# Output projection as seven block products, and the ends of the two down stages reordered, in a one-core decoder block

## The chip, the cores and the metric

The kernel runs on one core of a Trainium2 chip. The time is that of one execution on the device in microseconds (us); the profile is taken in one more execution by the hardware profiler. Lower is better. All arithmetic is float32 in value: each operand of a matrix product is split into a high part in the format fp32r and a low part, the rest, and a product is three matmuls (high by high, high by low, low by high).

## The reference

One decoder block over 512 tokens of 1024 features: a SwiGLU feed-forward, a token mixer, and a second SwiGLU feed-forward, each with an RMS norm before and after it and a residual. Cut to what matters:

```
f = swiglu(rms_norm(h, ffn1_pre_g), ffn1_w_gu, ffn1_w_down)        # d_ff 2816
h = h + 0.5 * rms_norm(f, ffn1_post_g)
u = rms_norm(h, mix_pre_g);  z = u @ w_in
y_lru = rg_lru(conv4(x_br)) * gelu(gate_br)
y_attn = sliding window attention (128) with sinks on rotary q, k
merged = sigmoid(g_lru) * (y_lru @ w_proj_lru) + sigmoid(g_attn) * (y_attn @ w_proj_attn)
h = h + rms_norm(merged @ w_out, mix_post_g)                       # w_out: 1024 x 1024
f = swiglu(rms_norm(h, ffn2_pre_g), ffn2_w_gu, ffn2_w_down)
out = h + 0.5 * rms_norm(f, ffn2_post_g)
```

The change concerns `merged @ w_out` with the norm, residual and next norm behind it, and the last pieces of the two products with `w_down`.

## The kernel before

**Weights.** `worder` lists all weight pieces (128 x 1024 float32) in the order of use. `wload` (L102) loads raw pieces on SP's queue up to three ahead; `wsplit` casts a piece on ACT (L109) and forms its low part on DVE (L110); `wget` hands out the next piece and splits two ahead.

**Down stages** (`down`; tiles f1X, f1Y, f1Q and f2X, f2Y, f2Q). The product of the feed-forward's inner features with `w_down` is computed as 2 x 2 blocks: tokens in two halves, columns in two halves, inner features in two halves, with seven block products instead of eight. Sums of weight blocks are formed ahead of time in DRAM by a copy on SP's queue and an adding transfer on POOL's (tile wsum); sums of operand blocks are formed on DVE. The products run in the order 1, 2, 3, 6, 5, 7, 4, each in pieces of two 128-row chunks by two token tiles. The end is written out by hand: product 7's last pieces, then per token tile a combination (L660), a square with accumulation (L492), the splits of the next weights, the first steps of two token tiles' epilogues, and product 4 per token tile.

**Boundary.** `boundary` makes the steps behind a product with `half` (a square with accumulation on ACT, the post gain on DVE, L496) and `epilogue`, a generator in steps: a mean (L506) and a power on POOL (L193) and late gains; the residual on DVE (L519) with squares on ACT (L524) and a store; a second mean and power; the next norm's scaling (L532); and `to_features`: eight transposes on PE (L208), casts on ACT (L212), low parts on DVE (L213), and raw copies on ACT (L217), which give the next stage's moving operands u. The last step runs a number of `tick` calls later (`FEATURE_LAG`).

**Output projection** (`token_out`; tiles woo). Eight chunks of 128 rows of `w_out`. The operand is the merged activation, split per chunk as soon as it is made (mgh, mgl; L1098 to L1102). All eight accumulator banks are in use (four token tiles by two halves of 512 columns). Chunk 0 goes over all banks; the other seven (`TAILS`) go token tile by token tile, so that each finished tile's epilogue runs while the next tile is multiplied. Then `gate_up` of the second feed-forward begins with `first_four` (tiles f2f): four weight pieces over tokens 0 to 255, then the same four over tokens 256 to 511.

**Order.** Inside `tc.manual_schedule()` each engine keeps the order in which the code issues. The down stages and the paired products are inside; the output projection and `first_four` are not, and there the order comes from a planner.

Of the kernel before, what the change touches and what calls it, by code (L numbers as in the profile page):

```python
# [16 lines left out]
P = 128  # L17
LRU_LAG = (2, 2)
ATT_LAG = (3, 2)
TAILS = 7  # L20
WARM = 10
JSTD = {"f1": 6, "f2": 4}
FEATURE_LAG = {"b1": (7, 9, 7, 3), "b2": (3, 3, 3, 3)}
# [19 lines left out]
def hybrid_block_kernel(ctx, tc, x, xt, g1, w_first, gains, gu1, gs1, dn1, w_x, w_gate, w_q, w_k, w_v, w_gl, w_ga, w_pl, w_pa,  # L43
# [27 lines left out]
    worder = []  # L71
    caps = []
    wsum = {}
    for gu, dn in ((gu1, dn1), (gu2, dn2)):
        worder += [gu[j, i] for j in range(gu.shape[0]) for i in range(2)]
        caps.append(len(worder))
        sums = [dram.tile([P, KS * 512], F32, name=f"wsum{len(wsum)}{i}") for i in range(4)]
        s1, s2, s3, s4 = sums
        wsum[len(wsum)] = (dn, sums)
        for w in (dn[0], dn[1], s4, s2, s1, s3, dn[3]):  # L80
            worder += [w[:, i:min(i + 1024, KS * 512)] for i in range(0, KS * 512, 1024)]
        if gu is gu1:
            worder += [w_x[c] for c in range(4)] + [w_k[i] for i in range(2)] + [w_v[i] for i in range(2)]
            worder += [w_x[c] for c in range(4, 8)] + [w_q[i] for i in range(4)]
            worder += [w_gate[c] for c in range(8)] + [w_q[i] for i in range(4, 8)]
            worder += [w[c] for c in range(8) for w in (w_gl, w_pl)]
            worder += [w[c] for c in range(8) for w in (w_ga, w_pa)]
            worder += [w_o[c] for c in range(8)]
    AHEAD = 2
    RAHEAD = [3]  # L90
    raws = []
# [10 lines left out]
            wdma.append(SP.dma_start(raw, worder[n]))  # L102
            raws.append(raw)

    def wsplit(upto):
        while len(wready) < min(upto, wcap[0]):
            n = len(wready)
            w = b8(f"w{n}", [P, 2, 1024], F32R)[:, :, :worder[n].shape[-1]]
            A.copy(w[:, 0, :], raws[n])  # L109
            V.tensor_tensor(out=w[:, 1, :], in0=raws[n], in1=w[:, 0, :].bitcast(F32),  # L110
                            op=ALU.subtract)
            wready.append((w[:, 0, :], w[:, 1, :]))
            wload(n + 1 + RAHEAD[0])

    def wget():
        i = wpos[0]
        wpos[0] += 1
        wsplit(i + 1 + AHEAD)
        return wready[i]

    live = []
# [314 lines left out]
            add(n - 1, 21)  # L436
            finish(n - 1)

    def token_out(chunk, n, finish, name, tail_n):
        half, epilogue, _ = finish  # L440
        banks = {}

        def block(t, c, w, i):
            ph, pl = chunks[c]
            ts_ = slice(t * P, (t + 1) * P)
            if (t, i) not in banks:
                banks[t, i] = bank(f"{name}o{t}{i}")
            ns = slice(i * 512, (i + 1) * 512)
            mm3(banks[t, i], ph[:, c % 4, ts_], pl[:, c % 4, ts_], w[0][:, ns], w[1][:, ns], c == 0, c == n - 1)

        chunks = {}
        tail = []
        for c in range(n):
            w = wget()
            chunks[c] = chunk(c)
            if c < n - tail_n:
                for t in range(NT):
                    for i in range(2):
                        block(t, c, w, i)
                tick()  # L460
            else:
                tail.append((c, w))
        for t in range(NT):
            for i in range(2):
                for c, w in tail:
                    block(t, c, w, i)
            for i in range(2):
                half(t, i, banks[t, i])
            start(epilogue(t))
            tick()  # L470

    def boundary(src, dst, g_post, g_pre, u, scale, name, raw=None, then=None):
# [12 lines left out]
        def half(t, i, z, sign=1.0, o=None):  # L485
            if t not in sq:
                sq[t], parts[t] = sm(f"{name}ps{t}", 2), [None, None]
# [4 lines left out]
            A.activation(t4(f"{name}sq{t}{i}")[:, :512], z, AF.Square, scale=1.0 / 32.0, accum_out=sq[t][:, i:i + 1])  # L492
            parts[t][i] = o

            def gain():
                V.scalar_tensor_tensor(out=o, in0=z, scalar=sign * scale, in1=g_post[:, cols[i]], op0=ALU.mult,  # L496
                                       op1=ALU.mult)

            if i == 0:
                gain()  # L500
            else:
                late[t] = gain

        def inverse(ms, z):
            me = sm(f"{name}{z}e")
            V.tensor_scalar(out=me, in0=ms[:, 0:1], scalar1=ms[:, 1:2], scalar2=EPS, op0=ALU.add, op1=ALU.add)  # L506
            return rstd(me, f"{name}{z}r")

        def epilogue(t):
            while len(rhs) < min(t + 2, NT):  # L510
                residual()
            res, h = rhs[t][:, 0, :], rhs[t][:, 1, :]
            r = inverse(sq[t], f"p{t}")
            late[t]()
            yield
            if g_pre is not None:
                ms, un = sm(f"{name}ms{t}", 2), t4(f"{name}un{t}")
            for i in range(2):
                V.scalar_tensor_tensor(out=h[:, cols[i]], in0=parts[t][i], scalar=r, in1=res[:, cols[i]],  # L519
                                       op0=ALU.mult, op1=ALU.add)  # L520
                if g_pre is None:
                    (SP if i == 0 else A).dma_start(dst[t][:, cols[i]], h[:, cols[i]])
                else:
                    A.activation(un[:, cols[i]], h[:, cols[i]], AF.Square, scale=1.0 / 32.0, accum_out=ms[:, i:i + 1])  # L524
            if g_pre is None:
                return
            A.dma_start(dst[t], h)
            yield
            r = inverse(ms, f"n{t}")
            yield  # L530
            for i in range(2):
                V.scalar_tensor_tensor(out=un[:, cols[i]], in0=h[:, cols[i]], scalar=r, in1=g_pre[:, cols[i]],  # L532
                                       op0=ALU.mult, op1=ALU.mult)
            yield FEATURE_LAG[name][t]
            to_features(un, t, u, f"{name}n", raw)
            if then is not None and t == NT - 1:
                start(then())

        return half, epilogue, residual

    def down(ps, name):
# [91 lines left out]
        with tc.manual_schedule():  # L633
# [18 lines left out]
                        V.tensor_tensor(out=sn["p"][t], in0=Q[t], in1=sn["p"][t], op=ALU.subtract)  # L652
            w = [wget(), wget()]
            prep[7][4]()
            for t in range(2):
                for c in range(KS - 3, KS):
                    unit(7, c, w[c // (KS - 1)], (t,))
# [5 lines left out]
            gens = [epilogue(t) for t in range(2)]  # L663
            for gen in gens:
                next(gen)
            wsplit(wpos[0] + (KS + 1) // 2)
            run(gens)
            ws = []
            for t in range(2):
# [385 lines left out]
    def next_attend(*a):  # L1055
        if todo:
            g, n = todo.pop(0)
            start(attend(g, n, kp, vt, y0 if g < 2 else y1))

    for c in range(KD):  # L1060
        gate_chunk(c)
        if c in ATT_GATES:
            next_attend()
    start(q_pair(2, next_attend))
# [13 lines left out]
    for c in range(KD):  # L1078
# [11 lines left out]
    start(split_y(y1, "ya1"))  # L1090
    while live:
        tick()
    mg = []
    for c in range(KD):
        s, b = sig_gate(c, ya, "ga")
        if c % 4 == 0:
            mg.append((b8(f"mgh{c}", [P, 4, T], F32R), b8(f"mgl{c}", [P, 4, T], F32R)))
        V.scalar_tensor_tensor(out=s, in0=s, scalar=1.0, in1=b, op0=ALU.add, op1=ALU.mult)  # L1098
        V.tensor_tensor(out=s, in0=s, in1=m1[c // 4][:, c % 4, :], op=ALU.add)
        mh, ml = mg[-1]  # L1100
        A.mul(mh[:, c % 4, :], s, 0.5)
        V.scalar_tensor_tensor(out=ml[:, c % 4, :], in0=s, scalar=0.5, in1=mh[:, c % 4, :].bitcast(F32),  # L1102
                               op0=ALU.mult, op1=ALU.subtract)

    g_post, g_pre = gain_pair(3, 2, "g_b2")
    u3 = new_u("u3")
    hs2 = [dram.tile([P, D], F32, name=f"h2_spill{t}") for t in range(NT)]
    raw3 = [b8(f"u3r{i}", [P, 4, T]) for i in range(2)]
    mv3 = {}
    finish = boundary(hs, hs2, g_post, g_pre, u3, 1.0, "b2", raw3, lambda: moving(raw3, "u3", mv3))  # L1110
    for _ in range(2):
        finish[2]()
    token_out(lambda c: mg[c // 4], KD, finish, "wo", TAILS)

    dn_run = []
    gate_up(u3, "f2", first_four, lambda: (gs2, blocks(u3, mv3)), begin(dn_run, "f2"))
# [7 lines left out]
def _layout(inputs):  # L1124
# [48 lines left out]
    a["w_o"] = c(f["w_out"].reshape(KD, P, D))  # L1173
# [41 lines left out]
```

## Time and profile before

| | |
|---|---|
| median of 3 runs | 1123.41 us (1123.25 to 1123.79) |
| profiled execution, its own time | 1123.8 us |
| its span, first to last instruction | 1122.0 us |
| granted TensorE clock, mean | 0.999 |
| busy: PE, weight loads, DVE, ACT, POOL | 1104.2, 982.2, 894.6, 591.2, 82.0 us |
| DMA moved | 202.07 MB, mean 180 GB/s |

PE is the matrix engine, PEld its weight loads, DVE the vector engine, ACT the scalar engine, POOL GpSimd, SP the queue engine for DMAs. A row of the timeline gives the start and the duration in us, engine, line of the kernel, operation, the tile written and the tiles read, shape and count, and in brackets how long the engine idled before it and what ended that. Rows of waits give engine, line and tile, what was waited for, then the total, the count and the longest in us. Rows of groups give after the bar the busy us, the mean ns of one, and the idle time before them. Matmuls are pipelined: their pace is the distance of their starts, not their duration.

### The profile page before, as it was taken

How to read it: one execution, taken by the hardware profiler on the slowest of the kernel's cores; microseconds unless marked ns; L12 is line 12 of the kernel's file. 1: busy time of each engine (PE TensorE's matmuls, PEld its weight loads, DVE VectorE, ACT ScalarE, POOL GpSimd, SP SyncE). 2: the span in 40 equal slices, each digit the busy share in tenths (PEclk: the TensorE clock that was granted, in tenths of full speed). 3: DMA queues.
4: the chain of work that ended last, by engine and by line, in shares of the span. 5: the costliest groups of instructions: out<-in, count | busy, mean ns of one | idle time of the engine just before them, and what ended most of it. 6: DMA issues, size and time to landing. Idle time of an engine off the chain costs nothing.

```text
span 1122.0 us, 16778 instructions
## 1 busy us (share of the span) xinstructions
PE 1104.2 (98%) x6558; PEld 982.2 (88%) x6558; DVE 894.6 (80%) x1277; ACT 591.2 (53%) x991; POOL 82.0 (7%) x82
## 2 busy tenths in 40 slices
PE   9999999999989999999999999999999999999997
PEld 7889999988878888888888888888999999998885
DVE  6998898888988788999777562546858888988895
ACT  7445555465665658566555351436435455556562
POOL 1000000000011001124112000001000000000001
PEclk9999999999999999999999999999999999999999
DMA  9239999664677272711823340623348999455473
GB/s 348 94 123 263 305 285 299 186 225 131 226 255 242 76 207 95 187 57 57 264 75 94 113 168 20 203 98 131 113 115 260 271 329 265 132 175 191 145 268 112
DMA packets 53280, 202.07 MB, mean 180 GB/s; under 512 B 6353, under 2 KB 6481, under 8 KB 48465
## 3 DMA queue, kind: packets, MB, share of 16 engines
q1 hardware_dynamic: 45424, 163.77, 43.4%
q0 software_dynamic: 3456, 23.07, 10.6%
q10 hardware_dynamic: 4320, 14.16, 3.5%
q8 instruction: 51, 0.84, 0.3%
q14 instruction: 29, 0.23, 0.1%
HBM read 189.44 MB, written 57.67 MB: 220 GB/s over the span
## 4 chain that ended last, share of the span: by engine, by line
PE 87%; DVE 7%; issue 2%; ACT 2%; DMA 1%; POOL 0%; SPq 0%; DVEq 0%; ACTq 0%; POOLq 0%
PE f2X L150 5%; PE f2X L149 5%; PE f2X L148 5%; PE f1X L150 4%; PE f1X L149 4%; PE f1X L148 4%; PE f2Q L149 2%; PE f2Q L148 2%; PE f2Q L150 2%; PE f1Q L149 2%; PE f1Q L148 2%; PE f1Q L150 2%; PE f1f L776 2%; DVE w L110 2%; PE glg L148 1%
## 5 line engine op out<-in xcount | busy, mean ns | idle before, releaser
L110 DVE TENSOR_TENSOR w<-wraw,w 128x1024 fp32r<-128x1024 f32 x168 | 196.9, 1193 | 36.9 <-ACT w L109 35.3
L109 ACT CAST w<-wraw 128x1024 fp32r<-128x1024 f32 x168 | 163.2, 1011 | 24.5 <-PE glp L150 7.4
L150 PE MATMUL f1X<-u1m,f1W 128*128 128x256 f32 x256 | 72.6, 283 | 0.1
L149 PE MATMUL f1X<-u1m,f1W 128*128 128x256 f32 x256 | 72.4, 283 | 0.0
L148 PE MATMUL f1X<-u1m,f1W 128*128 128x256 f32 x256 | 72.4, 283 | 0.0
L150 PEld LDWEIGHTS f1X<-u1m,f1W 128*128 128x128 f32 x256 | 49.1, 192 | 0.3 <-DVE f1W L319 0.3
L148 PEld LDWEIGHTS f1X<-u1m,f1W 128*128 128x128 f32 x256 | 49.1, 192 | 0.1
L149 PEld LDWEIGHTS f1X<-u1m,f1W 128*128 128x128 f32 x256 | 49.1, 192 | 0.1
L150 PE MATMUL f2X<-u3m,f2W 128*128 128x256 f32 x144 | 40.9, 284 | 0.1
L149 PE MATMUL f2X<-u3l,f2W 128*128 128x256 f32 x144 | 40.8, 283 | 0.0
L150 PE MATMUL f2X<-u3h,f2W 128*128 128x256 f32 x144 | 40.8, 283 | 0.0
L148 PE MATMUL f2Q<-u3m,f2W 128*128 128x256 f32 x144 | 40.8, 283 | 0.0
L149 PE MATMUL f2Q<-u3m,f2W 128*128 128x256 f32 x144 | 40.8, 283 | 0.0
L150 PE MATMUL f2Q<-u3m,f2W 128*128 128x256 f32 x144 | 40.8, 283 | 0.0
L148 PE MATMUL f2X<-u3m,f2W 128*128 128x256 f32 x144 | 40.7, 283 | 0.0
L149 PE MATMUL f2X<-u3m,f2W 128*128 128x256 f32 x144 | 40.7, 283 | 0.0
L148 PE MATMUL f2X<-u3h,f2W 128*128 128x256 f32 x144 | 40.7, 283 | 0.0
L148 PE MATMUL f1Q<-u1m,f1W 128*128 128x256 f32 x128 | 36.2, 283 | 0.0
L149 PE MATMUL f1Q<-u1m,f1W 128*128 128x256 f32 x128 | 36.2, 283 | 0.0
L150 PE MATMUL f1Q<-u1m,f1W 128*128 128x256 f32 x128 | 36.2, 283 | 0.0
L149 PE MATMUL f1X<-w,f1y 128*128 128x512 f32 x88 | 34.5, 392 | 1.7 <-DVE w L110 1.7
L149 PE MATMUL f2X<-w,f2y 128*128 128x512 f32 x88 | 34.5, 392 | 1.7 <-DVE w L110 1.7
(845 smaller groups left out, 3752.3 us busy)
## 6 DMA issues: line engine op xcount, KB each, us to landing
wraw<-wsum SPq DMA_DIRECT2D x40, 512.0 KB, 4.2
wsum<-in_dn_dram SPq DMA_DIRECT2D x16, 1024.0 KB, 9.9
wraw<-in_dn_dram SPq DMA_DIRECT2D x30, 512.0 KB, 4.8
f2L<-in_gs_dram SPq DMA_DIRECT2D x18, 512.0 KB, 5.0
f2R<-in_gs_dram SPq DMA_DIRECT2D x18, 512.0 KB, 5.3
wraw<-in_gu_dram SPq DMA_DIRECT2D x16, 512.0 KB, 5.4
f1L<-in_gs_dram SPq DMA_DIRECT2D x16, 512.0 KB, 5.8
f1R<-in_gs_dram SPq DMA_DIRECT2D x16, 512.0 KB, 5.5
```

What stands on the lines that cost most here:

```text
L109: A.copy(w[:, 0, :], raws[n])
L110: V.tensor_tensor(out=w[:, 1, :], in0=raws[n], in1=w[:, 0, :].bitcast(F32), op=ALU.subtract)
L148: PE.matmul(o, lhsT=ah, rhs=bh, start=start, stop=False, skip_group_check=reopen)
L149: PE.matmul(o, lhsT=ah, rhs=bl, start=False, stop=False, skip_group_check=reopen)
L150: PE.matmul(o, lhsT=al, rhs=bh, start=False, stop=stop, skip_group_check=reopen)
L776: PE.matmul(bs[i], lhsT=lw[:, i * P:(i + 1) * P], rhs=rx, start=k == 0 and n == 0, stop=k == KD - 1 and n == 2)
```

## The change

The output projection takes the down stages' form: 2 x 2 blocks with seven products of four 128-row chunks, two token tiles and three matmuls, in the order 1, 2, 6, 5, 3, 7, 4 (X, Y, Q are six of the eight banks). `w_out` is laid out anew on the host as four blocks without arithmetic. Four sums of its blocks are formed in DRAM: copies on SP's queue in the loop of `gate_chunk`, adding transfers on POOL's in the loop of the first merge gate. Operand blocks are split when they are needed (`oop_split`), their sums are formed on DVE. The merged activation is kept unsplit in mg. The stage is written out by hand in `tc.manual_schedule()`, with the epilogues of four token tiles interleaved, and with two weight pieces' low parts on POOL. `half` gets `wait`, which puts the gain into the epilogue, and `boundary` gets `unit`.

In the down stages the last four weight pieces are cast by `wround` ahead of product 7's last pieces, and the low parts of the last two alternate with the second steps of the two epilogues.

```
+    def wround(upto):
+        while len(whi) < min(upto, wcap[0]):
+            n = len(whi)
+            wload(n + 1)
+            w = b8(f"w{n}", [P, 2, 1024], F32R)[:, :, :worder[n].shape[-1]]
+            A.copy(w[:, 0, :], raws[n])
+            whi.append(w)
+    def wsplit(upto, eng=V):
+            wround(n + 1)
+            w = whi[n]
+            eng.tensor_tensor(out=w[:, 1, :], in0=raws[n], in1=w[:, 0, :].bitcast(F32), op=ALU.subtract)
...
     # down
             w = [wget(), wget()]
             prep[7][4]()
+            wround(wpos[0] + (KS + 1) // 2)
             for t in range(2):
                 for c in range(KS - 3, KS):
                     unit(7, c, w[c // (KS - 1)], (t,))
...
             for gen in gens:
                 next(gen)
-            wsplit(wpos[0] + (KS + 1) // 2)
+            for t, gen in enumerate(gens):
+                if next(gen, True) is not None:
+                    gens = []
+                wsplit(wpos[0] + (KS + 1) // 2 - 1 + t)
             run(gens)
...
+    oplan = ((0, 2, 0), (2, 3, 2), (1, 3, None), (3, 1, None))
     for c in range(KD):
         gate_chunk(c)
+        if c % 2 == 0:
+            o, a, _ = oplan[c // 2]
+            SP.dma_start(osum[o], w_o[a])
...
+        if c % 2 == 0:
+            o, _, b = oplan[c // 2]
+            G.dma_start(osum[o], osum[c // 2 - 2] if b is None else w_o[b], accum_op=ALU.add)
...
     for c in range(KD):
         s, b = sig_gate(c, ya, "ga")
         V.scalar_tensor_tensor(out=s, in0=s, scalar=1.0, in1=b, op0=ALU.add, op1=ALU.mult)
+        V.tensor_tensor(out=mg[c // 4][:, c % 4, :], in0=s, in1=m1[c // 4][:, c % 4, :], op=ALU.add)
+        if c == 4:
+            oop_split(1, a11)
+        if c == 5:
+            oop_split(7, osum_tile("os3", a11, a21, ALU.subtract))
+            oop_split(2, a12, ks=slice(0, 2))
...
     # token_out, in tc.manual_schedule()
+        product(1, first_sums, next_sum)
+        snap("a", X)
+        for _ in range(2):
+            residual()
+        product(2, lambda: oop_split(6, S[2], -1.0), lambda: osum_tile("os4", S[2], a12, ALU.subtract, S[2]))
+        for t in range(2):
+            plus("a", Y, t)
+            half(t, 0, sn["a"][t])
+        product(6, lambda: oop_split(5, S[1]), lambda: oop_split(3, S[2]))
+        snap("u", X)
+        product(5, lambda: oop_split(4, a22))
+        snap("q", Q)
+        product(3, lambda: None, lambda: wsplit(wpos[0] + 4))
+        u3.extend(new_u("u3"))
+        raw3.extend(b8(f"u3r{i}", [P, 4, T]) for i in range(2))
+        for t in range(2):
+            plus("u", Q, t)
+            half(t, 1, sn["u"][t], -1.0)
+        e = [epilogue(t) for t in range(NT)]
+        for t in range(2):
+            next(e[t])
+        w = [wnow() for _ in range(2)]
+        for t in range(2):
+            for k in range(4):
+                unit(7, k, w[k // 2], (t,))
+            if t == 1:
+                next(e[0])
+                next(e[1])
+                next(e[0])
+                wsplit(wpos[0] + 3)
+                next(e[1])
+            plus("q", X, t)
+            half(2 + t, 1, sn["q"][t], -1.0, sn["q"][t], True)
+        w = [wnow() for _ in range(2)]
+        next(e[0])
+        next(e[1])
+        for k in range(4):
+            unit(4, k, w[k // 2], (0,))
+        half(2, 0, X[0])
+        for n in range(2):
+            for k in (2 * n, 2 * n + 1):
+                unit(4, k, w[n], (1,))
+            next(e[n], None)
+        half(3, 0, X[1])
+        wsplit(wpos[0] + 2)
+        next(e[2])
+        next(e[2])
+        wsplit(wpos[0] + 4, G)
+        next(e[3])
+        next(e[3])
+        next(e[2])
+        next(e[3])
+        for t in (2, 3):
+            live.append([e[t], next(e[t])])
```

More of the change, by code (lines that the diff above doesn't have):

```diff
@@ L19 @@
 ATT_LAG = (3, 2)
-TAILS = 7
 WARM = 10
@@ L73, in hybrid_block_kernel @@
     wsum = {}
+    osums = dram.tile([P, 4, 4 * 512], F32, name="osums")
+    osum = [osums[:, i, :] for i in range(4)]
     for gu, dn in ((gu1, dn1), (gu2, dn2)):
@@ L87, in hybrid_block_kernel @@
             worder += [w[c] for c in range(8) for w in (w_ga, w_pa)]
-            worder += [w_o[c] for c in range(8)]
+            t1, t2_, t3, t4_ = osum
+            for w in (w_o[0], w_o[1], t2_, t1, w_o[3], t3, t4_):
+                worder += [w[:, i:i + 1024] for i in (0, 1024)]
     AHEAD = 2
@@ L103, in wload @@
             raws.append(raw)
-    def wsplit(upto):
+    whi = []
+    def wround(upto):
[6 more added lines that the diff above has]
+    def wsplit(upto, eng=V):
         while len(wready) < min(upto, wcap[0]):
             n = len(wready)
-            w = b8(f"w{n}", [P, 2, 1024], F32R)[:, :, :worder[n].shape[-1]]
-            A.copy(w[:, 0, :], raws[n])
-            V.tensor_tensor(out=w[:, 1, :], in0=raws[n], in1=w[:, 0, :].bitcast(F32),
+            wround(n + 1)
+            w = whi[n]
+            eng.tensor_tensor(out=w[:, 1, :], in0=raws[n], in1=w[:, 0, :].bitcast(F32),
                             op=ALU.subtract)
@@ L118, in wget, with wnow @@
         wsplit(i + 1 + AHEAD)
+        return wready[i]
+    def wnow():
+        i = wpos[0]
+        wpos[0] += 1
+        wsplit(i + 1)
         return wready[i]
@@ L437, in paired, with boundary @@
             finish(n - 1)
[L439 to L472, printed above, removed]
+    def boundary(src, dst, g_post, g_pre, u, scale, name, raw=None, then=None, unit=1.0):
         rhs = []
@@ L483, in boundary, with half @@
         sq, parts, late = {}, {}, {}
-        def half(t, i, z, sign=1.0, o=None):
+        def half(t, i, z, sign=1.0, o=None, wait=False):
             if t not in sq:
-                sq[t], parts[t] = sm(f"{name}ps{t}", 2), [None, None]
+                sq[t], parts[t], late[t] = sm(f"{name}ps{t}", 2), [None, None], []
+                wait = wait or i == 1
+            else:
+                wait = True
             if o is None:
@@ L491, in half @@
                 o = rhs[t][:, 1, cols[i]]
-            A.activation(t4(f"{name}sq{t}{i}")[:, :512], z, AF.Square, scale=1.0 / 32.0, accum_out=sq[t][:, i:i + 1])
+            A.activation(t4(f"{name}sq{t}{i}")[:, :512], z, AF.Square, scale=unit / 32.0, accum_out=sq[t][:, i:i + 1])
             parts[t][i] = o
             def gain():
-                V.scalar_tensor_tensor(out=o, in0=z, scalar=sign * scale, in1=g_post[:, cols[i]], op0=ALU.mult,
-                                       op1=ALU.mult)
-            if i == 0:
+                V.scalar_tensor_tensor(out=o, in0=z, scalar=sign * scale * unit, in1=g_post[:, cols[i]],
+                                       op0=ALU.mult, op1=ALU.mult)
+            if wait:
+                late[t].append(gain)
+            else:
                 gain()
-            else:
-                late[t] = gain
         def inverse(ms, z):
@@ L513, in epilogue @@
             r = inverse(sq[t], f"p{t}")
-            late[t]()
+            for gain in late[t]:
+                gain()
             yield
@@ L1092, in hybrid_block_kernel, with oop_new, oop_split @@
         tick()
-    mg = []
+    mg = [b8(f"mg{i}", [P, 4, T]) for i in range(2)]
+    lo_, hi_ = slice(0, 256), slice(256, 512)
+    a11, a21, a12, a22 = (mg[i][:, :, tok] for i in range(2) for tok in (lo_, hi_))
+    oop = {}
+    def oop_new(i):
+        oop[i] = b8(f"oy{i}", [P, 2, 4, 256], F32R)
+        return oop[i]
+    def oop_split(i, z, sign=1.0, ks=slice(0, 4)):
+        o = oop[i] if i in oop else oop_new(i)
+        if sign == 1.0:
+            A.copy(o[:, 0, ks], z[:, ks])
+            V.tensor_tensor(out=o[:, 1, ks], in0=z[:, ks], in1=o[:, 0, ks].bitcast(F32), op=ALU.subtract)
+        else:
+            A.activation(o[:, 0, ks], z[:, ks], AF.Copy, scale=sign)
+            V.scalar_tensor_tensor(out=o[:, 1, ks], in0=z[:, ks], scalar=sign, in1=o[:, 0, ks].bitcast(F32),
+                                   op0=ALU.mult, op1=ALU.subtract)
@@ L1094, in hybrid_block_kernel, with osum_tile @@
+    def osum_tile(name, a, b, f, o=None):
+        if o is None:
+            o = t4(name).rearrange("p (k t) -> p k t", k=4)
+        V.tensor_tensor(out=o, in0=a, in1=b, op=f)
+        return o
     for c in range(KD):
         s, b = sig_gate(c, ya, "ga")
-        if c % 4 == 0:
-            mg.append((b8(f"mgh{c}", [P, 4, T], F32R), b8(f"mgl{c}", [P, 4, T], F32R)))
         V.scalar_tensor_tensor(out=s, in0=s, scalar=1.0, in1=b, op0=ALU.add, op1=ALU.mult)
-        V.tensor_tensor(out=s, in0=s, in1=m1[c // 4][:, c % 4, :], op=ALU.add)
@@ L1100, in hybrid_block_kernel @@
[L1100 to L1103, printed above, removed]
+        V.tensor_tensor(out=mg[c // 4][:, c % 4, :], in0=s, in1=m1[c // 4][:, c % 4, :], op=ALU.add)
[4 more added lines that the diff above has]
+            oop_split(2, a12, ks=slice(0, 2))
@@ L1105, in hybrid_block_kernel, with token_out, unit, product @@
     g_post, g_pre = gain_pair(3, 2, "g_b2")
-    u3 = new_u("u3")
     hs2 = [dram.tile([P, D], F32, name=f"h2_spill{t}") for t in range(NT)]
[L1108 to L1113, printed above, removed]
+    raw3, u3, mv3 = [], [], {}
+    def token_out():
+        X, Y, Q = ([bank(f"wo{z}{t}") for t in range(2)] for z in "XYQ")
+        dst = {1: X, 2: Y, 6: X, 5: Q, 3: Q, 7: X, 4: X}
+        half, epilogue, residual = boundary(hs, hs2, g_post, g_pre, u3, 1.0, "b2", raw3,
+                                            lambda: moving(raw3, "u3", mv3), 0.5)
+        def unit(i, k, w, tiles):
+            y, n = oop[i], k % 2 * 512
+            for t in tiles:
+                ts_ = slice(t * P, (t + 1) * P)
+                mm3(dst[i][t], y[:, 0, k, ts_], y[:, 1, k, ts_], w[0][:, n:n + 512], w[1][:, n:n + 512],
+                    k == 0 and i in (1, 2, 5), k == 3, True)
+        def product(i, *prep):
+            for n in range(2):
+                w = wget()
+                if n < len(prep):
+                    prep[n]()
+                for k in (2 * n, 2 * n + 1):
+                    unit(i, k, w, range(2))
+        sn = {}
+        def snap(key, z):
+            sn[key] = [t2(f"wo{key}{t}") for t in range(2)]
+            for t in range(2):
+                A.copy(sn[key][t], z[t])
+        def plus(key, z, t):
+            V.tensor_tensor(out=sn[key][t], in0=z[t], in1=sn[key][t], op=ALU.add)
+        S = {}
+        def first_sums():
+            oop_split(2, a12, ks=slice(2, 4))
+            S[1] = osum_tile("os1", a22, a21, ALU.subtract)
+        def next_sum():
+            S[2] = osum_tile("os2", S[1], a11, ALU.add)
+        product(1, first_sums, next_sum)
[20 more added lines that the diff above has]
+        w = [wnow() for _ in range(2)]
+        for t in range(2):
+            for k in range(4):
[14 more added lines that the diff above has]
+        half(2, 0, X[0])
+        for n in range(2):
+            for k in (2 * n, 2 * n + 1):
+                unit(4, k, w[n], (1,))
[11 more added lines that the diff above has]
+            live.append([e[t], next(e[t])])
@@ L1115, in hybrid_block_kernel @@
+    with tc.manual_schedule():
+        token_out()
     dn_run = []
@@ L1172, in _layout @@
     a["w_pa"] = chunks(wa)
-    a["w_o"] = c(f["w_out"].reshape(KD, P, D))
+    w = f["w_out"].reshape(2, 4, P, 2, 512)
+    a["w_o"] = c(np.stack([w[j, :, :, i].transpose(1, 0, 2).reshape(P, 2048) for i in range(2) for j in range(2)]))
     a["gu2"], a["gs2"] = gu(f["ffn2_w_gu"])[:JSTD["f2"]], pairs_of(f["ffn2_w_gu"], JSTD["f2"])
```

## The prediction

> **What bounds the kernel now.** I read the page's shares first, then the chain that ended last, then the rows of the waits of PE, and then the timeline of the three places where those waits lie. From the page:
>
> ```profile
> PE 1104.2 (98%) x6558; PEld 982.2 (88%) x6558; DVE 894.6 (80%) x1277; ACT 591.2 (53%) x991; POOL 82.0 (7%) x82
> ...
> PE 87%; DVE 7%; issue 2%; ACT 2%; DMA 1%; POOL 0%; SPq 0%; DVEq 0%; ACTq 0%; POOLq 0%
> ```
>
> PE is busy for 98% of the span and carries 87% of the chain. So a removed matmul is worth its full pace wherever nothing else is late, and a wait of PE costs its full length. The waits of PE that bear on the change:
>
> ```profile
> PE b1ntp L208 <- DVE b1un L532: 1.8, 2, 1.5
> PE f1X L149 <- DVE w L110: 1.7, 2, 0.9
> PE f2X L149 <- DVE w L110: 1.7, 2, 0.9
> ...
> PE f2f L148 <- ACT u3h L212: 1.2, 1, 1.2
> PE at02t L990 <- POOL at02s L984: 1.2, 1, 1.2
> ...
> PE f2f L149 <- DVE u3l L213: 0.5, 1, 0.5
> ```
>
> Four of them stand at the ends of the two down stages and two at the seam between output projection and second feed-forward. These are the places that the change edits. All are small, so what the change can win is a few matmuls and about 5 us of waits.
>
> **Part one: the ends of the down stages.** The second feed-forward's end, from the timeline (start, duration, engine, line):
>
> ```profile
> 1096.89 0.63 ACT L492 ACTIVATE b3sq<-f2p 128x512 f32<-128x512 f32 x1 [4.36 <-DVE f2p L660]
> ...
> 1097.52 1.04 ACT L109 CAST w<-wraw 128x1024 fp32r<-128x1024 f32 x1
> ...
> 1098.59 1.23 DVE L110 TENSOR_TENSOR w<-wraw,w 128x1024 fp32r<-128x1024 f32 x1 [1.79 <-ACT w L109]
> ...
> 1101.80 0.39 PE L150 MATMUL f2X<-w,f2y 128*128 128x512 f32 x1
> ...
> 1102.23 0.50 PE L148 MATMUL f2X<-w,f2y 128*128 128x512 f32 x1
> ...
> 1103.49 0.50 PE L149 MATMUL f2X<-w,f2y 128*128 128x512 f32 x1 [0.76 <-DVE w L110]
> ...
> 1104.75 0.40 PE L148 MATMUL f2X<-w,f2y 128*128 128x512 f32 x1
> 1104.80 1.82 DVE L110 TENSOR_TENSOR w<-wraw,w 128x1024 fp32r<-128x1024 f32 x2
> 1106.07 0.50 PE L149 MATMUL f2X<-w,f2y 128*128 128x512 f32 x1 [0.92 <-DVE w L110]
> 1106.54 1.40 DVE L519 SCALAR_TENSOR_TENSOR b3rh<-b3rh,b3p0r 128x512 f32<-128x512 f32 x2
> ...
> 1108.05 0.39 PE L148 MATMUL f2X<-w,f2y 128*128 128x512 f32 x1
> ```
>
> ACT idles 4.36 us, then squares the first finished tile and only afterwards casts the next weight piece. DVE idles 1.79 us for that cast, and PE loses 0.20, 1.03 and 1.09 us: each matmul below starts that much more than its pace of 0.23 after the one above it (1102.23, 1103.49 and 1106.07), 2.3 us in all. `wround` puts the four casts (three of about 1 us, one half) into the 4.36 us of ACT's idle time. DVE then goes through its fixed order without idling: from the end of product 7's first tile at 1095.91, the subtractions for pieces 3 and 4 end at 1097.9 and 1100.0, two small steps and two gains end at 1101.6, the first tile's pair of L519 takes 1.40, and the subtraction for piece 5 ends at 1104.1, the second pair 1.40, the half piece's at 1106.1. PE, not held before, wants piece 5's low part at 1103.6 and piece 6's at 1105.6: it waits 0.3 to 0.6 at each instead of 2.3. The matmul of 1108.05 comes at 1106.6: **minus 1.5 us**. Should the last two casts find no free buffer before product 7 ends, ACT is held until then, and the squares behind them come some 2 us later; DVE's first use of these squares is at 1100, so it costs 0 to 0.7. Ends for this term: minus 0.8 to minus 2.3.
>
> The first feed-forward's end is the same code with one more wait behind it:
>
> ```profile
> 335.10 0.39 PE L150 MATMUL f1X<-w,f1y 128*128 128x512 f32 x1
> ...
> 336.15 1.40 DVE L532 SCALAR_TENSOR_TENSOR b1un<-b1rh,b1n0r,g_b 128x512 f32<-128x512 f32 x2
> ...
> 336.95 1.32 PE L208 MATMUL b1ntp<-ident,b1un 128*128 128x128 f32 x8 [1.46 <-DVE b1un L532]
> ```
>
> PE stands from 335.33 to 336.95, and 0.3 more between the two groups of four transposes. In DVE's new order L532 starts at 332.9 instead of 336.15, PE gets to the transposes at 333.9, and the wait goes: 1.5 plus 1.7, **minus 3.2 us**. What follows is a chain through DVE, which moves with it. Ends: minus 1.5 to minus 3.5. Both ends together: minus 4.7.
>
> **Part two: the output projection.** Rows that carry it:
>
> ```profile
> 732.24:776.66 44.42, 44.42 (x201) 36.82 (x200) 21.70 (x35) 15.32 (x35) 3.30 (x6) 1.00 0.22 82
> ```
>
> ```profile
> 776.66 1.03 PE L208 MATMUL b2ntp<-ident,b2un 128*128 128x128 f32 x8
> ...
> 778.94 0.39 PE L148 MATMUL f2f<-u3h,w 128*128 128x256 f32 x1 [1.24 <-ACT u3h L212]
> ...
> 780.83 0.39 PE L149 MATMUL f2f<-u3l,w 128*128 128x256 f32 x1 [0.51 <-DVE u3l L213]
> ...
> 786.45 1.03 PE L208 MATMUL b2ntp<-ident,b2un 128*128 128x128 f32 x8
> 787.24 0.36 PE L148 MATMUL f2f<-u3h,w 128*128 128x256 f32 x1
> ...
> 804.59 0.40 PE L148 MATMUL f2g<-u3h,w 128*128 128x512 f32 x1
> ```
>
> The first row is a stretch (length, then busy time of PE, weight loads, DVE, ACT, POOL). It holds 192 matmuls and eight transposes; the transposes take 0.79 (787.24 less 786.45), so a matmul goes at 0.227. Seven products of 24 make 168: 24 fewer, **minus 5.4 us** at PE. The price is on DVE, which had 21.7 busy us of 44.4. Costs of one step, with row:
>
> ```profile
> 729.29 4.63 DVE L110 TENSOR_TENSOR w<-wraw,w 128x1024 fp32r<-128x1024 f32 x4 [0.20 <-ACT w L109]
> 728.22 5.05 ACT L109 CAST w<-wraw 128x1024 fp32r<-128x1024 f32 x5
> ```
>
> A wide DVE step goes at 1.14 ((4.63 less one of 1.22) over 3), a half step at 0.68, an ACT cast at about 1.0. I count time from 732.24 as 0 and lay the new code's order out on each engine, each step waiting for what it reads.
>
> From 0 to the fifth product DVE has: the last merge chunk 1.4; twelve weight subtractions (14 pieces now instead of 8 chunks, two done ahead) 13.7; the low parts of operands 2 (half), 6, 5, 3, 4, 5.2; three operand sums 3.4; four sums and gains for the first block 2.7: 26.4 us, and 2.9 of waits for ACT, which casts in the same order and stands behind each accumulator copy and square. DVE is through at 29.3. PE needs 120 matmuls, 27.2, and waits 1.2 at the fourth product (operand 5's low part is ready at 18.0): 28.4. So DVE, with ample slack before, becomes the bound here by 0.9 us.
>
> Then DVE has in its queue: two sums, gains, the sum of product 7's first tile (ends 33.1), four residual steps (to 35.8), one weight subtraction that waits for ACT's cast behind four squares (37.65 to 38.8), and only then the sum for product 7's second tile, which ends at 39.6. Product 4's second tile writes the bank that this sum reads. PE is there at 36.6 and **waits 3.0**. Product 4 ends at 43.2 with one set of transposes inside; before, it was 44.4 (776.66). Of the 5.4 us, 4.2 are gone. The first block matmul follows at 45.0, with 0.6 more for the low part: before 46.7 and 0.75.
>
> The rest is what the new order puts last. Before, each token tile ended 42 matmuls, 9.5 us, ahead of the next; now the last two end within 3.5 us, and ahead of their steps stand weights that the next stage needs at once. ACT copies the first two tiles until 47.0, squares, casts; the second weight is split at 49.8 (PE waits 1.2). Tile 2's gains and residual end at 52.7. Then two weight subtractions go to POOL, whose queue also holds the small powers of tile 3 and of both normalisations. POOL's rows:
>
> ```profile
> L984 POOL TENSOR_TENSOR at11s<-at11s,at11ss 128x1024 f32<-128x1024 f32 x1 | 2.8, 2837 | 10.5 <-DVE at11ss L983 10.5
> L193 POOL TENSOR_TENSOR b3p1r<-b3p1e,mhalf 128x1 f32<-128x1 f32 x1 | 2.5, 2456 | 0.0
> ...
> L984 POOL TENSOR_TENSOR at03s<-at03s,at03ss 128x1024 f32<-128x1024 f32 x1 | 1.9, 1898 | 2.1 <-DVE at03ss L983 2.1
> ...
> L923 POOL TENSOR_TENSOR q0m<-q0m,q0m 128x512 f32<-128x512 f32 x1 | 1.3, 1304 | 45.5 <-DVE q0m L921 45.5
> ```
>
> No row has a plain 128x1024 subtraction on POOL. The low end is 1.9 (at03s, whose second operand is one broadcast column). The high end is 3.5: twice the plain half-width step q0m, 2.6, and 0.9 more, which at11s lost against at03s. I take the row that is nearest in size and surroundings, at11s with 2.8: DVE is otherwise idle there for 5 us, and the free schedule behind the hand-written one will fill that with other subtractions. POOL starts at 54.6 behind the casts and ends at 60.2; PE waits 1.9 and 2.7 for these two weights. Tile 3's power follows, then its residual, squares, two powers and both tiles' last DVE steps, done at 65.9; transposes and copies, and the second half of the block starts at 66.5 with 1.3 for its low part. With 96 matmuls at 0.12 the block ends at 79.3. Before: 804.59, or 72.35. Net **plus 7.0 us** (5.2 at 1.9 and 8.4 at 3.5, since both subtractions stand one behind the other).
>
> Here the row b3p1r shows a one-column power stretched from 0.55 to 2.46 while DVE ran the L110 pair of 1104.80. [...]
>
> The weight sums: four 1 MB copies on SP's queue and four adding transfers on POOL's. The page has the same kind:
>
> ```profile
> wsum<-in_dn_dram POOLq DMA_DIRECT2D x8, 1024.0 KB, 10.0
> ```
>
> They depend on nothing but weights and are read 100 us later, so I cost them at nothing, covered by a DMA share of 0.2 to 0.4. If one stood on POOL before an attention step, the wait at02t of 1.2 could grow by 0.8 each: ends 0 and 1.6. A 512 KB piece each 2.7 us is the pace that the down stages already keep.
>
> **Sum.** The profiled execution took 1123.8 (span 1122.0 and 1.8 around it), 0.4 above the median of 1123.41. 1123.8 less 4.7 plus 7.0 is 1126.1; against the median 1125.7. I say 1125.8. About 0.2%, 2.2 us, is what a measurement of this kernel tells from no change.
>
> **Rivals.** First, faster: POOL's two subtractions are not in the chain of tile 3, since the power gets ahead of them or they are long done. The chain then ends some 6 us earlier, the block at 73.0, plus 0.7 instead of 7.0, and the time is 1119.8; with DVE's queue also 4 us shorter it is 1115.5. It decides from where the last b2un ends before 61 on my count (793 in the old times). For it: PE's count falls without question. Against it: manual order is kept strictly, as DVE's 1.79 idle ahead of L110 shows.
>
> Second, no visible change: subtractions at 1.9, seam plus 5.2, tails minus 4.7: 1124.3.
>
> Third, slower by more: new buffers are short (two sums, raw pieces and squares share eight), or POOL and DVE lock each other twice: 3 to 6 us on top, 1129 to 1132.
>
> **How the numbers follow.** The worked case, 1124.3 to 1127.5 by POOL's price, has 0.57, 0.33 of it above the 0.2% line and 0.24 within; the faster one 0.26, of which 0.02 within; the third 0.17. Slower 0.50, same 0.26, faster 0.24. For 8 in 10 the range takes nearly all of the faster case and most of the third: 1115 to 1131; the worked case alone is 1124 to 1128.
>
> **What would show it.** Tails: no L109 between the squares; PE's waits for L110 near 0.5 each; b1ntp without a wait. Seam: woo ends about 1 us earlier, not 5; a PE wait of about 3 us there for a DVE sum; POOL rows for w of 2 to 3 us; f2f waiting for POOL and for u3h. If those waits are missing and PE's busy share stays, I am wrong on the faster side.

## The result, and the profile after

The changed kernel takes 1137.16 us (median of 4 runs, 1135.86 to 1138.57) against 1123.6 before, timed beside it: ratio 1.0119, 95% interval 1.0104 to 1.0134, some 13.5 us slower. The forecast was 1125.8, between 1115 and 1131. The profiled execution took 1136.34, its span 1134.4, 12.4 more than before. Where it went is read by the start of the same matmuls in both traces (f1X and f2X belong to the two feed-forwards' paired products and down stages, x is the mixer's first product, f2f the second feed-forward's first):

| stretch | before | after | more |
|---|---|---|---|
| to the first f1X (start of the kernel) | 72.48 | 78.78 | +6.3 |
| first f1X to first x (holds the first down stage's end) | 273.2 | 269.6 | -3.6 |
| first x to the projection's first matmul | 386.6 | 387.0 | +0.5 |
| projection to first f2f | 46.7 | 45.1 | -1.6 |
| first f2f to first f2X | 47.4 | 60.0 | +12.6 |
| first to last f2X (holds the second down stage's end) | 288.9 | 287.4 | -1.6 |

**The start.** Timeline of before, SP's queue, then of after, SP's queue, ACT and PE (start, duration, engine, line, operation; in brackets the idle time and what ended it):

```profile
15.94 6.97 SPq L102 DMA_DIRECT2D wraw<-in_gu_dram  x5
```

```profile
15.48 4.33 SPq L1059 DMA_DIRECT2D osums<-in_w_o_dram  x4
20.67 5.30 SPq L105 DMA_DIRECT2D wraw<-in_gu_dram  x4
...
49.17 1.04 ACT L115 CAST w<-wraw 128x1024 fp32r<-128x1024 f32 x1 [10.73 <-DMA wraw<-in_gu_dram]
...
50.27 0.50 PE L167 MATMUL f1g<-u1h,w 128*128 128x512 f32 x1 [4.46 <-ACT w L115]
...
50.85 0.63 PE L169 MATMUL f1g<-u1h,w 128*128 128x512 f32 x1
```

The four copies of `w_out` blocks, which the code issues in the gate stage 400 us later, stand in SP's queue ahead of the first feed-forward's weights: they depend on nothing, and outside the hand-written schedule the planner took them forward. Four adding transfers follow. Stretches of before and of after (columns: length, busy us of PE, weight loads, DVE, ACT, POOL, granted clock, DMA share, GB/s):

```profile
28.00:42.00 14.00, 14.00 (x67) 11.70 (x66) 12.28 (x18) 6.28 (x8) 0.00 (x0) 1.00 0.14 56
42.00:56.00 14.00, 14.00 (x64) 11.58 (x63) 14.00 (x16) 6.34 (x8) 0.00 (x0) 1.00 0.45 132
```

```profile
28.00:42.00 14.00, 14.00 (x67) 11.71 (x66) 12.36 (x18) 2.79 (x4) 1.82 (x2) 1.00 1.03 282
42.00:56.00 14.00, 9.54 (x35) 7.38 (x34) 7.20 (x9) 4.14 (x5) 1.62 (x2) 0.88 1.02 277
```

The DMA engines are full until 66 us (share 1.02 to 1.03 from 14 to 66 us), ACT waits 10.73 us for a weight, PE 4.46, and for 3.4 us behind that wait the matmuls go at 0.43 instead of 0.23 (50.85 to 54.25, eight matmuls). The wait and the 1.6 us that the slow matmuls lose make 6.1 of the 6.3 us.

**The seam.** The waits of PE after (engine, line, tile, what was waited for: total us, times, longest):

```profile
PE b2ntp L227 <- DVE b2un L522: 3.0, 1, 3.0
PE woX L167 <- DVE woq L1162: 2.3, 1, 2.3
PE f2f L169 <- POOL w L123: 1.9, 1, 1.9
PE f2f L167 <- ACT w L115: 1.6, 1, 1.6
...
PE f2X L168 <- DVE w L123: 0.4, 2, 0.3
...
PE f1X L168 <- DVE w L123: 0.4, 2, 0.3
PE b1ntp L227 <- DVE b1un L522: 0.3, 1, 0.3
```

The last three are the down stages' ends: 1.7, 1.7 and 1.8 before. The first four lie in the seam: b2un are a token tile's scaled rows ahead of the transposes, woq is the sum behind product 7, w a weight piece of the next stage. The longest of them, for b2un, ends the chain of the last token tile (tile 3), here from DVE, POOL and PE:

```profile
789.76 5.68 POOL L123 TENSOR_TENSOR w<-wraw,w 128x1024 fp32r<-128x1024 f32 x2 [3.49 <-ACT w L115]
791.61 4.91 DVE L123 TENSOR_TENSOR w<-wraw,w 128x1024 fp32r<-128x1024 f32 x2 [2.31 <-ACT w L115]
795.40 1.53 POOL L212 TENSOR_TENSOR b2p3r<-b2p3e,mhalf 128x1 f32<-128x1 f32 x1
796.96 0.75 DVE L509 SCALAR_TENSOR_TENSOR b2rh<-b2rh,b2p3r 128x512 f32<-128x512 f32 x1 [0.44 <-POOL b2p3r L212]
...
800.20 3.65 PE L227 MATMUL b2ntp<-ident,b2un 128*128 128x128 f32 x16 [2.97 <-DVE b2un L522]
803.50 0.56 PE L167 MATMUL f2f<-u3h,w 128*128 128x256 f32 x1
```

Tile 3's power waits for POOL's two low parts, and DVE meanwhile makes two later weights' low parts at twice their 1.22 us. The granted clock is halved there:

```profile
788.00:792.00 4.00, 0.60 (x3) 0.30 (x2) 1.69 (x4) 4.00 (x8) 2.24 (x1) 0.94 0.35 135
792.00:796.00 4.00, 3.83 (x18) 3.83 (x19) 4.00 (x2) 0.53 (x1) 4.00 (x3) 0.50 0.00 0
796.00:800.00 4.00, 1.23 (x6) 0.94 (x5) 2.88 (x7) 1.34 (x4) 2.01 (x3) 0.50 0.67 210
800.00:804.00 4.00, 3.80 (x18) 3.83 (x19) 3.69 (x7) 2.14 (x5) 0.46 (x1) 0.50 0.30 88
```

### The profile page after: what moved, and what is told of

Its sections match the earlier page's. It is cut to its first block, busy times and chain, and to the rows that moved or that the text cites. A ratio compares the mean times of both kernels' runs of the same rounds, so it can differ in the third digit from the quotient of the medians.

```text
span 1134.4 us, 16780 instructions
## 1 busy us (share of the span) xinstructions
PE 1106.3 (98%) x6534; PEld 983.1 (87%) x6534; DVE 913.5 (81%) x1291; ACT 602.4 (53%) x1003; POOL 89.2 (8%) x88
## 5 line engine op out<-in xcount | busy, mean ns | idle before, releaser
L123 DVE TENSOR_TENSOR w<-wraw,w 128x1024 fp32r<-128x1024 f32 (+1 forms) x172 | 205.0, 1211 | 40.3 <-ACT w L115 38.4
L115 ACT CAST w<-wraw 128x1024 fp32r<-128x1024 f32 x174 | 169.4, 1012 | 40.1 <-DMA wraw<-in_gu_dram 14.1
L1121 DVE SCALAR_TENSOR_TENSOR gas<-gas,gap 128x512 f32<-128x512 f32 x8 | 5.5, 688 | 45.2 <-PE gap L169 45.2
```

The costliest lines, as they stand in the source:

```text
L123: eng.tensor_tensor(out=w[:, 1, :], in0=raws[n], in1=w[:, 0, :].bitcast(F32), op=ALU.subtract)
```

## The experiments

All start from the changed kernel but b_tails. Times are medians of device time (before lay between 1123.6 and 1124.3), ratios stand to the kernel before, with 95% intervals. "Seam" is the projection's first matmul to the first f2X in the profile, as two stretches divided by the first f2f.

| kernel | us | ratio | seam |
|---|---|---|---|
| before | 1123.8 | 1 | 46.7 + 47.4 |
| after | 1137.16 | 1.0119 [1.0104, 1.0134] | 45.1 + 60.0 |
| a_pin | 1136.49 | 1.0118 [1.0098, 1.0138] | 46.5 + 59.5 |
| a_pin3 | 1129.78 | 1.0051 [1.0036, 1.0066] | 45.1 + 59.9 |
| b_tails | 1118.89 | 0.9954 [0.9940, 0.9969] | 46.7 + 47.4 |
| a_dve | 1130.56 | 1.0063 [1.0046, 1.0080] | 46.6 + 54.9 |
| a_pin_dve | 1132.65 | 1.0084 [1.0066, 1.0101] | 46.5 + 54.9 |
| a_pin3_dve | 1124.58 | 1.0007 [0.9997, 1.0016] | 45.1 + 54.9 |
| a_plus | 1136.50 | 1.0109 [1.0092, 1.0126] | 44.9 + 60.4 |
| a_fill | 1135.75 | 1.0102 [1.0087, 1.0117] | 45.1 + 59.5 |
| a_late | 1125.44 | 1.0014 [1.0004, 1.0024] | 46.5 + 57.4 |
| a_order | 1125.05 | 1.0010 [1.0000, 1.0019] | 46.8 + 53.8 |
| a_order2 | 1118.72 | 0.9953 [0.9939, 0.9968] | 44.0 + 50.2 |
| a_order3 | 1117.71 | 0.9943 [0.9930, 0.9957] | 42.4 + 50.6 |

**Where the transfers stand.** a_pin holds each copy behind the weight load ahead of it in the code, and each add behind the attention multiply ahead of it on POOL:

```
+            with tc.issue_after(wdma[-1].ins):
+                SP.dma_start(osum[o], w_o[a])
...
+            with tc.issue_after(gq[-1].ins):
+                G.dma_start(osum[o], ..., accum_op=ALU.add)
```

> The changed kernel with the four weight-sum copies held behind the weight load that the program text puts ahead of them, and the four adding transfers held behind the attention multiply ahead of them; nothing else. Theory (the copies, issued at 15.5 us ahead of the first in_gu loads, cost the start 6.3 us): first f1X matmul back at 72.5 us from 78.8, granted clock 1.00 in 48 to 54 us, median 1131 us (1130 to 1132), ratio to before 1.0065. Rival (the eight transfers cost their traffic or their queue slots wherever they stand): the 6.3 us turn up as waits in the gate and attention stages, median 1134 to 1137.

The rival's number came. The start was mended (first f1X at 72.2), as the theory said, but the time did not move, since the transfers now met the query halves (tile qt, loaded for the attention): the stretch from the first x to the projection took 392.5 us instead of 387.0. PE's longest wait and a stretch of a_pin:

```profile
PE at20b L961 <- DMA qt<-q_halves: 3.6, 1, 3.6
...
530.00:560.00 30.00, 26.44 (x122) 21.92 (x121) 18.45 (x28) 11.93 (x17) 2.53 (x2) 0.94 0.89 251
```

The code's own place was no better than the planner's. Whether it is so "wherever they stand", a_pin3 tells. It moves them on: copies in the fifth and seventh chunk of the first merge gate (the expectation counts them one too high) and the first and third of the second, adds behind the last attention multiply.

> The changed kernel with the eight weight-sum transfers moved to the last third of the gate stages: copies held behind weight loads of the sixth and eighth linear-gate chunk and of the first and third attention-gate chunk, all four adds behind the last attention multiply on POOL. Theory (a transfer of these costs only where it meets another that PE is near to waiting for: the first weights at 50 us, or the query halves at 548 us): first f1X at 72.3, no wait for qt over 1.5 us, woX about 728.8, median 1130.5 us (1129.5 to 1132). Rival (8 MB more are a burden wherever they lie): a new wait of 3 us or more for a gate weight between 590 and 730 us, 1134 to 1137.

The theory held: f1X at 72.3, projection from 728.6 (735.4), and no wait beyond before's between: 7.4 us less. With the right place the transfers cost nothing that can be seen. All later runs bear it out: the four profiles with the copies in front (the changed kernel, a_dve, a_plus, a_fill) reach the first f1X at 78.8 to 80.3 us, the eight with them moved at 71.6 to 72.9.

**The ends of the down stages alone.** b_tails is the kernel before with `wround` and the interleaved splits:

```
+            wround(wpos[0] + (KS + 1) // 2)
...
-            wsplit(wpos[0] + (KS + 1) // 2)
+            for t, gen in enumerate(gens):
+                if next(gen, True) is not None:
+                    gens = []
+                wsplit(wpos[0] + (KS + 1) // 2 - 1 + t)
```

> The kernel before with only the down stages' tails of the change (last pieces cast ahead of the accumulator reads, their low parts between the epilogues). Theory (the tails give 3.6 and 1.57 us on their own): median 1118.4 us (1117.5 to 1119.5), ratio 0.9954. Rival (the gain of the first tail was only time that the late start had put there, since the changed kernel reached that stage 6.3 us later with the same loads): 1121 to 1122, only the second tail's 1.6 us.

As the theory had it: f1X to x 269.6 us (273.2 before), first to last f2X 287.3 (288.9).

**POOL in tile 3's chain.** a_dve makes the two low parts on DVE behind tile 3's residual; a_pin_dve and a_pin3_dve add the moved transfers.

```
-        wsplit(wpos[0] + 4, G)
+        wround(wpos[0] + 4)
         next(e[3])
         next(e[3])
+        wsplit(wpos[0] + 4)
```

> The changed kernel with the two low parts that POOL made (5.68 us, between tile 2's and tile 3's power) made on DVE behind tile 3's residual instead, their casts ahead of tile 3's squares. Theory (POOL's 5.68 us stand in tile 3's chain, and DVE's two splits beside them run at double length): tile 3's power at about 789 us instead of 795.4, last b2un done at 796 instead of 802.0, median 1130.5 us (1129.5 to 1132.5). Rival (the seam is held by the late weight casts and by the half clock, not by POOL): the clock stays at 0.50 there, and the median falls by less than 2 us, 1135 to 1137.

> Both edits, the pinned transfers and the two low parts on DVE. Theory (two causes at two places, additive): 1124.5 us (1123 to 1126), ratio 1.001. Rival (one of them only moves the wait): as the better of the two alone, 1130 to 1132.

> The transfers in the last third of the gate stages and the two POOL low parts on DVE, both as measured alone (-7.4 and -6.6 us against the changed kernel's 1137.2). Theory (two causes at two places, additive): 1123.2 us (1122 to 1124.5), woX to f2X 101.6 us. Rival (part of the -6.6 was the later start of that run's stage): 1125 to 1127.

a_dve gained 6.6 us; PE's 3.0 of wait for b2un is gone, though the clock still falls (from 795.2 us its matmuls start 0.21 apart instead of 0.12). Its profiled execution is the longest of its four (1133.84, with half pace behind the wait for woq), so the profile shows less than the median. a_pin_dve missed its 1124.5, for the reason that a_pin shows. a_pin3_dve came 1.4 above the sum of the two, just over its range and under its rival's. The seam's second stretch is 54.9 in all three, so the gain there is 5.1 us, which is also what a_pin3_dve has over a_pin3 (5.2).

a_late leaves POOL its low parts and takes only DVE's two splits out of that time (with the transfers as in a_pin3):

```
-            first.append((wget(), bank(f"{name}{i}")))
+            first.append(((wnow if name == "f2f" else wget)(), bank(f"{name}{i}")))
```

> The changed kernel with the transfers in the last third of the gate stages and, in the seam, the splits of f2 weights five and six behind the chain, so that DVE has nothing to do while POOL makes its two low parts (against 1129.8 us with only the transfers moved). If POOL and DVE exclude each other (DVE's two splits took 4.91 us there instead of 2.4): POOL's pair takes 3.4 to 4.2 us instead of 5.68, b2un comes 2 us earlier, 1127.5 to 1128.5. If only DVE is slowed by POOL: POOL's pair keeps 5.7 us, 1129.5 to 1130.5.

```profile
784.22 4.68 POOL L123 TENSOR_TENSOR w<-wraw,w 128x1024 fp32r<-128x1024 f32 x2 [3.49 <-ACT w L115]
788.86 0.55 POOL L212 TENSOR_TENSOR b2p3r<-b2p3e,mhalf 128x1 f32<-128x1 f32 x1
```

Each engine slowed the other: with DVE idle, POOL's pair takes 4.68 instead of 5.68 and the power 0.55 instead of 1.53; DVE's pair took 4.91 beside POOL's and takes 2.35 in a_dve, where POOL has none. The pair's forecast (3.4 to 4.2) was too low, the time's (1127.5 to 1128.5) too high. The profiled execution is the longest of ten (1127.93), with a drop of the clock behind its wait for woq (starts 0.43 apart instead of 0.23) that the median may not have, and its seam's first stretch is some 1.5 us longer than a_pin3's. So 4.3 us of gain are measured, of which the seam's second stretch shows 2.5 and the whole seam 1.1; where the rest came is not shown.

**One wait of PE, and the clock.** a_plus moves the sum for product 7's second tile ahead of the second residual:

```
                 next(e[0])
+            plus("q", X, t)
+            if t == 1:
                 next(e[1])
                 next(e[0])
                 wsplit(wpos[0] + 3)
                 next(e[1])
-            plus("q", X, t)
```

> The changed kernel with one step moved: the sum for product 7's second tile stands behind the first tile's residual on DVE, ahead of the second residual, a weight split and two small steps. Theory (PE's 2.3 us wait for it is a matter of DVE's order, but tile 3's chain sets the end of the seam): the wait woX for woq goes, f2f starts 2 us earlier, and 1.0 to 2.3 us of that last to the end: 1135 us (1134.5 to 1136.2). Rival (what follows on DVE and POOL is late anyway): the wait turns up at f2f and b2ntp, 1136.5 to 1137.5.

The rival was right by the seam, 105.3 us against 105.1 (the four times scatter over 3.6 us). PE's wait for woq is gone and another stands in its place, in PE's waits of a_plus:

```profile
PE b2ntp L227 <- DVE b2un L522: 5.4, 2, 3.6
```

a_fill puts matmuls that compute nothing into three waits; their results are overwritten:

```
+        for _ in range(9):
+            PE.matmul(Y[0], lhsT=oop[4][:, 0, 0, :P], rhs=w[0][0][:, :512], start=True, stop=True)
```

> The changed kernel with matmuls that compute nothing put into three waits of PE in the seam: 9 of 128x512 ahead of product 4's second tile, 28 of 128x256 ahead of the third f2f weight, 22 ahead of the third tile's transposes. Theory (the granted clock falls because PE idles, and only then): the clock stays at 1.00 from 770 to 808 us, the 16 transposes take 1.7 us instead of 3.3, the waits of DVE, ACT and POOL stay as they are, median 1134.5 us (1133.5 to 1136). Rival (the clock falls for another reason, the work of the other engines or the transfers, or it costs nothing as the chain runs through POOL and DVE): 0.50 again, 1136.5 to 1139.

```profile
792.00:796.00 4.00, 3.46 (x29) 3.26 (x28) 3.63 (x2) 1.27 (x2) 4.00 (x2) 1.00 0.00 0
796.00:800.00 4.00, 2.50 (x21) 2.30 (x20) 2.88 (x5) 1.33 (x4) 2.28 (x3) 1.00 0.41 131
800.00:804.00 4.00, 2.98 (x15) 2.78 (x16) 4.00 (x7) 1.52 (x3) 1.00 (x2) 0.69 0.46 139
```

With PE kept at work the clock stays at 1.00 from 784 to 800 us, so its fall there is the waits' doing. Behind 800 us, where the theory had 1.00 too, it falls to 0.69, behind a wait of 2.4 us that was left. The time lies in the theory's range, but the seam is only 0.5 us shorter, and the 1.4 us of the median lie within the two kernels' scatter: the half clock sits mostly beside POOL's chain. It explains less of the loss than its rows suggest.

**The order of the seam.** a_order (with a_pin3's transfers) puts product 7's sums as soon as its tiles end, works tile 2's epilogue between product 4's halves, and has no low part on POOL:

```
         half(2, 0, X[0])
+        wsplit(wpos[0] + 1)
+        next(e[2])
...
             next(e[n], None)
+            if n == 0:
+                next(e[2])
         half(3, 0, X[1])
```

> The transfers as in the third-of-gate-stage version, and the seam's order on DVE, ACT and POOL rewritten: product 7's sums as soon as its tiles end, tile 2's power, gains and residual between product 4's halves, the splits of the first four f2 weights on DVE behind the chain steps that are due, none on POOL. Theory (what the seam loses is the order of the work around the seven products, not the products): last b2un by 789 us less 4 for the earlier start of the stage, no granted clock under 0.9, woX to f2X 94 to 98 us (105.1 in the changed kernel, 94.1 before), median 1119.5 us (1117 to 1122). Rival (two tiles that end together leave too little cover, whatever the order): 100 us or more, 1123 to 1126.

By its numbers the rival had it, for a reason that neither named: tile 2's steps now stand ahead of tile 1's features. In the code's order DVE makes a low part of tile 0's features behind a weight split and tile 2's gains, and ACT squares tile 2's residual (1.2 us) ahead of casting tile 1's features (u3h), for which PE waits 4.6 us.

```profile
PE f2f L167 <- ACT u3h L231: 4.6, 1, 4.6
PE b2ntp L227 <- DVE b2un L522: 2.2, 1, 2.2
```

a_order2 casts the features first, the first two weights before them, and takes a_late's edit in; a_order3 also holds the plain copies of the features until both tiles' casts are done, and casts the second weight behind those casts.

```
-        next(e[2])
+        wround(wpos[0] + 2)
...
-            if n == 0:
-                next(e[2])
         half(3, 0, X[1])
         wsplit(wpos[0] + 2)
+        next(e[2])
+        wround(wpos[0] + 3)
+        next(e[2])
         next(e[3])
...
+        if name == "b2n" and t == 0:
+            return
```

> As the rewritten order of the seam, but with the casts of the first tiles' features ahead of tile 2's squares on ACT, the first two weights cast early, and the splits of weights five and six behind the chain. Theory (order of the work, not the cover, is what the seam loses; the rewritten order had put ACT's squares of tile 2 ahead of u3h, 4.6 us of wait): no wait for u3h over 1 us, f2f at 773.5, b2un done at 786 to 788, woX to f2X 95 to 98 us, 1119.5 us (1117.5 to 1122). Rival (too little cover behind two tiles that end together): b2ntp waits 4 us or more for b2un, 100 us, 1124 to 1126.

> As the second rewritten order (1118.7 us), with the plain copies of the first tile's features held until both tiles' casts are done, and the second f2 weight cast behind those. Theory (what is left in the seam is a wait of 1.85 us for u3h and the 3.6 us at a lowered clock that follow it): the wait shrinks to 1.3 us or less, the clock stays at 1.00 behind it, f2f at 771.0, 1116.7 us (1115.5 to 1118), below the kernel with only the tails (1118.9). Rival (DVE is busy without a pause from 768 to 785 us and sets when tile 3's b2un comes): f2f comes earlier, b2ntp waits that much longer for b2un, 1118 to 1119.5.

PE's waits of a_order3:

```profile
PE b2ntp L229 <- DVE b2un L530: 1.0, 1, 1.0
PE f2f L169 <- DVE w L123: 0.9, 1, 0.9
PE f2f L168 <- DVE u3l L234: 0.7, 1, 0.7
```

So the seam was lost by the order of the work and by the engine it stood on: 12 us of the changed kernel's 105 lay between two arrangements of the same work, with a_late's edit and the move of POOL's two low parts to DVE (5.1 us in a_dve) in it. Both forecasts of the time held (1119.5 and 1116.7, measured 1118.7 and 1117.7); a_order2 missed its sign for u3h (a wait of 1.85 us, not under 1), and a_order3 came with part of its rival's: f2f comes earlier, and b2ntp waits 1.0 for b2un instead of 0.7. In a_order3 the clock is 1.00 throughout the seam, which takes 93.0 us against 94.1 before: 1.1 us are kept of the 5.4 that the 24 matmuls fewer save. Its median is 1.2 under b_tails', with overlapping intervals and not timed side by side: whether the seven products win anything over the kernel with only the tails is open.

## Why the prediction was wrong, point by point

The stretches of the result make up the difference: minus 5.2 at the ends of the two down stages (forecast minus 4.7), plus 11.0 in the seam (plus 7.0), plus 6.3 at the start (nothing), and 0.5 between.

- **Part one held.** Minus 3.2 was 3.6, just past its end of 3.5; minus 1.5 was 1.6; b_tails shows both alone. (Of the six rows of waits shown there, three stand at the ends of the down stages, not four.)
- **"I cost them at nothing" failed: the weight sums.** Plus 6.3 to 7.4 us in its place. The prediction asked when the sums are read, and at which DMA share. It did not ask where the planner may put transfers that wait for nothing, although the section on the kernel before names the planner for what stands outside the hand-written schedule; and it put a price on a place in POOL's queue alone, not on one in SP's, ahead of the first weights. A rival that puts them there was not on the list.
- **The product stage held.** First block matmul 1.7 earlier, measured 1.6. The wait of 3.0 for the sum was 2.3. Its price was misread: a_plus shows it to be worth nothing while the chain behind stays.
- **Tile 3's chain held on its own engines.** POOL at 54.6 to 60.2, measured 54.4 to 60.0 from the stage's start; last b2un at 65.9, measured 66.6. The price of 2.8 for a subtraction held with DVE's pair beside it (5.68 for two); with DVE idle one took 2.34 (a_late).
- **The end of the block, plus 7.0, was mis-sized: it measured 11.0.** The forecast had all four weights' first halves ahead of the second half and 96 matmuls left at 66.5. The trace has 120 left at 68.1: the planner put the fourth weight's first half behind the 16 transposes (24 matmuls, 2.9 us), and transposes and the first matmuls ran at half clock (3.3 us for the transposes; before, half as many took 0.79). The block ends at 83.3, not 79.3.
- **POOL and DVE at the same time.** The prediction shows one such meeting, the power b3p1r; its sum has no term for one beyond the 2.8. Against a_late the meeting cost POOL's pair 1.0 (5.68 for 4.68) and the power behind it another 1.0 (1.53 for 0.55); it cost DVE's pair 2.5 (4.91 for twice 1.2). Taken one by one, the changed kernel's four subtractions and the power end one behind the other, at 792.1 (POOL), 793.2 (DVE), 795.4 (POOL), 796.5 (DVE) and 796.9 us (the power). Alone the two pairs take 4.68 and twice 1.2, 7.1 in all; together they took 6.8 from first start to last end, near their sum and not near the longer one.
- **The third rival** (buffers short, engines locking each other twice) named the right side but not the cause. Its 3 to 6 us were the author's estimate, worked out from no run; its locking was there (POOL's pair 5.68 for 4.68, DVE's 4.91 for twice 1.2), but inside the price of 2.8. With the transfers well placed, the change would have come out at 1129.8, inside the range, though 4 above the forecast and in this rival's band: the end of the block alone would not have broken the range.

## What to carry over

A transfer that depends on nothing has no place of its own in a planned schedule: look up where it is issued, and cost it at every place where it can land, against the transfers that the matrix engine is nearest to waiting for (here the first weights, 6.3 us, and the query halves, 5.5). The shorter product stage moved its cost to the engines that finish it (1.6 us won to the first f2f, 12.6 lost behind it): write the order of casts, squares, sums and small powers by who is waited for next, and keep bulk work off a queue that holds a one-column step of the last tile (5.1 us of the seam in a_dve). A single wait of the matrix engine that was taken away won nothing while a chain behind it was late (a_plus: 2.3 us of wait gone, the seam 105.3 us for 105.1).

## What the runs showed of the hardware

Behind the waits of PE of 2.9 us or more whose matmuls are listed one by one, they went at half pace: for 3.4 us behind 4.46 in the changed kernel, for 4.9 behind 2.97 there, for 4.5 behind 2.95 in a_pin3 (ahead of the last two they already did). Behind single waits of some 1.5 us and less they did not (1.36 us in the changed kernel, 1.46 before, 1.53 in a_order3). Between the two it was open. The wait of 2.3 us for woq was followed by half pace in four profiles (a_pin, a_dve, a_pin_dve, a_late; the seam's first stretch took 46.5 to 46.6 us) and not in three (the changed kernel, a_pin3, a_pin3_dve; 45.1 us); 1.85 us in a_order2 and 1.91 us in a_late were. Two waits of 1.6 and 1.8 to 1.9 us with two matmuls between them were, in the changed kernel, a_pin3, a_dve, a_pin3_dve and a_late (starts 0.21 us apart instead of 0.12). What decides it in between, no run shows.
